# Attention of a hybrid decoder trunk: 128-column value products at the diagonal, and one split of the joined heads for each pair

## The chip, the cores and the metric

The kernel runs on one core of a Trainium2 chip. The metric is the device time of one launch in microseconds; lower is better. The engines are called PE (TensorE, matrix products), PEld (its weight loads), DVE (VectorE), ACT (ScalarE), POOL (GpSimd) and SP (SyncE, which issues the transfers here).

## The reference

Two layers, each with a token mixer and an MLP, on 1024 positions of width 1024. The part that matters here is the forgetting attention: 8 heads of width 64, a causal softmax with a bias made of running sums of the forget gates, and the product with the values.

```
def block(args):
    i, q_i, c_i = args
    scores = jnp.einsum('bqhd,bkhd->bhqk', q_i, k).astype(jnp.float32) * scale
    bias = c_i[..., :, None] - c[..., None, :]
    q_pos = i * Q_BLOCK + jnp.arange(Q_BLOCK)
    causal = key_pos[None, :] <= q_pos[:, None]
    logits = jnp.where(causal, scores + bias, -jnp.inf)
    p = jax.nn.softmax(logits, axis=-1)
    return jnp.einsum('bhqk,bkhd->bqhd', p.astype(v.dtype), v)
```

Beside it each layer has four heads of retention (a linear recurrence in chunks of 128), a joint output projection, two layer norms and an MLP of width 4096 with a squared ReLU. Everything is float32.

## The kernel before

A product of two float32 operands is made of three products in the type fp32r, a rounded float32: `split(hi, lo, src)` (L158) writes the rounded value with ACT (L161, a cast) and the rest with DVE (L162, a subtraction), and the three products hi·hi, hi·lo and lo·hi are added up in PSUM. Splitting an operand therefore costs one ACT and one DVE instruction.

A layer runs in stages: the value projection, retention, the projection of queries and keys, attention, the output projection, the MLP. The attention stage stands at about 315 to 492 us in layer 0 and at about 1515 to 1690 us in layer 1. In each layer it covers the 8 heads one after the other, each in 4 steps `qq` of 256 query rows, so a layer has 32 steps. Beside the steps runs other PE work as a filler (`take`): 18 items for each of the first 24 steps, the projections of queries and keys for the later pairs of heads, then 4 for each step, among them the transposes of the retention's result (`ret_transposes`, L488, tile `rl`). Within a stage `merge` interleaves three generators, and a scheduler then sets each engine's order; every engine works through its own queue in that order.

For a step, `front` makes the scores of two blocks of 128 rows (PE L541 and, for the causal mask, L545), adds the bias and takes the minimum (DVE L547), applies exp (ACT L553), takes the reciprocal of the sum (DVE L555) and normalises the probabilities in place (POOL L556, tile `sc`). `load_bias` loads the running sums of a head (SP L513, tile `ncb`, one buffer) and derives `ref` (POOL L515); `bias` makes the bias tile `rel` (POOL L522). So POOL carries `ref`, `rel` and `sc`.

`back` (L560) turns the probabilities: for two key blocks and two query blocks PE transposes four 128x128 blocks into one PSUM tile `tr` (L569), and `split` makes from it the pair `pt` (hi and lo, 128 partitions x 4 blocks, three buffers of each). At the diagonal one of the four blocks lies wholly above it. It is not transposed: the key blocks are taken in the other order, so that it becomes block 0, and POOL writes zeros there (L574, once for hi and once for lo). `values` (L580) then runs 2 key blocks x 2 halves (hi, lo), four matmuls of 256 columns (L592), five tiles later than `back`. Values are kept as hi and lo side by side, 64 + 64 columns of the stationary operand, so that one half of the PSUM partitions has the product with hi and the other that with lo. At the end of each second step both halves are joined: ACT copies one (L603), DVE adds the other (L604, tile `ot`), and `split` writes the 64 partitions of this head into `mix`, the operand of the output projection. Two heads make a pair, which fills 128 partitions of `mix`.

Of the kernel before, what the change touches and what calls it, by code (L numbers as in the profile page):

```python
# [9 lines left out]
F32 = mybir.dt.float32  # L10
# [7 lines left out]
P = 128  # L18
# [4 lines left out]
RH, RD = 4, 128  # L23
# [52 lines left out]
def hybrid_trunk(ctx: ExitStack, tc, x, w_in, w_out, w_ff1, w_ff2, ln1_g, ln1_b, ln2_g, ln2_b,  # L76
                 b_forget, ret_gn_g, cst_d, rope_d, out):
    nc = tc.nc
    A, V, G, PE, SP = nc.scalar, nc.vector, nc.gpsimd, nc.tensor, nc.sync
# [43 lines left out]
    def nm(s):  # L123
        uid[0] += 1
        return f"{s}_{uid[0]}"
# [33 lines left out]
    def split(hi, lo, src, scale=1.0):  # L159
        if scale == 1.0:  # L160
            A.copy(hi, src)  # L161
            V.tensor_tensor(lo, src, hi.bitcast(F32), op=ALU.subtract)  # L162
        else:
            A.mul(hi, src, scale)
            V.scalar_tensor_tensor(lo, src, scale, hi.bitcast(F32), op0=ALU.mult, op1=ALU.subtract)
# [85 lines left out]
    def transpose_in(dst, src, tt, groups=2, banks_of=None):  # L251
        for g in range(groups):
            if banks_of is None:
                tr = ps_tr.tile([P, 4, P], F32, tag="tr", name=nm("tr"))
            else:
                tr = banks_of().rearrange("p (a b) -> p a b", b=P)
            for j in range(4):
                PE.transpose(tr[:, j, :], src[:, (4 * g + j) * P : (4 * g + j + 1) * P], ident)
            o = (tt % 4) * P
            split(dst.tile(0, g, tt // 4)[:, :, o : o + P], dst.tile(1, g, tt // 4)[:, :, o : o + P], tr)  # L260
# [226 lines left out]

    def ret_transposes(mr, pool):  # L488
        for tt in range(NT):
            t = pool.tile([P, RH * RD], F32, tag="rl", name=nm("rl"), bufs=1)  # L490
            SP.dma_start(t, r_d[tt * P : tt * P + P, :])
            transpose_in(mr, t, tt, groups=1)
            yield

    def attention(pool, mixes, fill, need, take):
        pv, heads, sums, rels, pvq = {}, {}, {}, {}, []

        def load(h):
            qs = pool.tile([P, S], F32R, tag="qs", name=nm("qs"), bufs=2)
# [60 lines left out]
        def back(h, qq, probs):  # L560
            for jp in range(qq + 1):
                diag = jp == qq
                tr = ps_tr.tile([P, 4, P], F32, tag="tr", name=nm("tr"))
                js = (2 * jp + 1, 2 * jp) if diag else (2 * jp, 2 * jp + 1)
                for i, j in enumerate(js):
                    for rb in range(2):
                        if diag and i == 0 and rb == 0:
                            continue
                        PE.transpose(tr[:, 2 * i + rb, :], probs[rb][:, j * P : j * P + P], ident)  # L569
                pt = [pool.tile([P, 4, P], F32R, tag=f"pt{a}", name=nm("pt"), bufs=PT_BUFS) for a in range(2)]  # L570
                f = 1 if diag else 0
                if diag:
                    for a in range(2):
                        G.memset(pt[a][:, 0, :].bitcast(F32), 0.0)  # L574
                split(pt[0][:, f:4, :], pt[1][:, f:4, :], tr[:, f:4, :])
                pvq.append((h, qq, jp, js, pt))
                yield
                if len(pvq) > LAG:
                    values(*pvq.pop(0))
                    yield  # L580

        def values(h, qq, jp, js, pt):
            p, e = h // 2, h % 2
            diag = jp == qq
            hq = qq // 2
            if (h, hq) not in pv:
                pv[(h, hq)] = ps_pv.tile([P, 512], F32, tag="pv", name=nm("pv"))
            ob = pv[(h, hq)]
            vp = heads[h][2]
            for i, j in enumerate(js):  # L590
                for b in range(2):
                    PE.matmul(ob[:, (qq % 2) * 256 : (qq % 2) * 256 + 256], vp[:, j, :], pt[b][:, 2 * i : 2 * i + 2, :],  # L592
                              start=qq % 2 == 0 and jp == 0 and i == 0 and b == 0,
                              stop=qq % 2 == 1 and diag and i == 1 and b == 1)
            if qq % 2 == 1 and diag:
                if p not in mixes:
                    mixes[p] = act.tile([P, 2, S], F32R, tag="act", name=nm("mix"))
                m = mixes[p]
                own = slice(64 * e, 64 * e + 64)
                oth = slice(64 - 64 * e, 128 - 64 * e)  # L600
                hs = slice(512 * hq, 512 * hq + 512)
                ot = pool.tile([P, 512], F32, tag="ot", name=nm("ot"), bufs=1)
                A.copy(ot[own], ob[oth])  # L603
                V.tensor_tensor(ot[own], ot[own], ob[own], op=ALU.add)  # L604
                split(m[own, 0, hs], m[own, 1, hs], ot[own])

        steps = [(h, qq) for h in range(FH) for qq in range(4)]
        def merge(gens):
# [20 lines left out]
        for i, st in enumerate(steps):  # L629
            h, qq = st  # L630
            n = fill(h, qq)
            if h + 1 < FH:
                if qq == 0:
                    if h % 2 == 1:
                        need((h + 1) // 2)
                    load(h + 1)
                if qq == 3 - DEPTH:
                    load_bias(h + 1)
            gens = [(2 * (qq + 1), back(h, qq, probs[st]))]
            if i + DEPTH < len(steps):  # L640
                nx = steps[i + DEPTH]
                gens.append(fronts(nx, probs[nx]))
            if n:
                gens.append((n, take(n)))
            merge(gens)
            if i + DEPTH + 1 < len(steps):
                bias(*steps[i + DEPTH + 1])
        while pvq:
            values(*pvq.pop(0))

    def layer(l, xT, nxt):
# [44 lines left out]
        with tc.tile_pool(name=f"p2_{l}", bufs=1, reuse_waits="tile") as pool:  # L696
            def rest():
                for p in range(1, FH // 2):
                    yield from project_qk(l, p, xT, pool)
                yield from ret_transposes(mr, pool)  # L700

            work = rest()

            done = [0, 0.0]

            def fill(h, qq):
                done[1] += FILL[h] * (qq + 1) / 10
                return max(0, int(done[1]) - done[0])

            def take(n):  # L710
                for _ in range(n):
                    done[0] += 1
                    next(work, None)
                    yield

            def need(p):
                while done[0] < QK_STEPS * p:
                    done[0] += 1
                    next(work, None)

            attention(pool, mix, fill, need, take)
            for _ in work:
                pass
# [453 lines left out]
```

## Time and profile before

| | us |
|---|---|
| median of 3 runs | 2420.84 (2418.31 to 2422.09) |
| the profiled execution | 2424.44 |
| its span, first to last instruction | 2422.6 |
| PE busy | 2364.4 (98%) |
| DVE busy | 1520.2 (63%) |
| ACT busy | 1025.1 (42%) |
| POOL busy | 359.3 (15%) |

The mean granted clock of TensorE in the profiled execution is 0.996. Two views are read below beside the totals: windows, which give each engine's busy time in a stretch, and timelines, which list an engine's instructions in order, with the idle time before each in brackets and what ended it. A group of several instructions stands in one row with its count; its duration is then from the first start to the last end.

### The profile page before, as it was taken

The numbers are of one execution on the slowest core, as the hardware profiler recorded it, in microseconds if no ns is written. First come the engines' busy times: TensorE is split into PE (matmuls) and PEld (weight loads), VectorE is DVE, ScalarE is ACT, GpSimd is POOL, SyncE is SP. The second block draws the span as 40 slices with busy tenths as digits, with TensorE's granted clock in tenths as the row PEclk, the third lists the DMA queues.
The fourth block names the chain that finished last, engine by engine and source line by source line (L and its number), as shares of the span: only waits on it lengthen the run. The fifth ranks groups of instructions, "written<-read, shape, count | busy, mean of one in ns | idle before, by whom it ended". The sixth has DMA issues, their size and how long they took to land. (4 is left out here: it accounts for less than half of the span.)

```text
span 2422.6 us, 32508 instructions
## 1 busy us (share of the span) xinstructions
PE 2364.4 (98%) x11888; PEld 1984.5 (82%) x11888; DVE 1520.2 (63%) x2719; ACT 1025.1 (42%) x1572; POOL 359.3 (15%) x597
## 2 busy tenths in 40 slices
PE   8999998999999999999999999989999999999997
PEld 8888877787888888888898888877878888888886
DVE  4655446854876667665655553587557766576557
ACT  3222245744644453434321212477264444543331
POOL 0232234510000000000202322354000000000003
PEclk9999999999999999999999999999999999999999
DMA  7565765533354458677545567654334544586663
GB/s 232 175 217 196 234 201 150 138 114 121 100 193 178 148 187 289 219 208 220 188 157 187 209 213 237 181 166 114 118 105 148 185 167 161 206 292 216 198 193 147
DMA packets 243808, 442.48 MB, mean 183 GB/s; under 512 B 26032, under 2 KB 128432, under 8 KB 235456
## 3 DMA queue, kind: packets, MB, share of 16 engines
q1 hardware_dynamic: 241344, 432.01, 54.9%
q10 hardware_dynamic: 2304, 8.39, 0.8%
q8 instruction: 94, 1.54, 0.3%
q14 instruction: 66, 0.54, 0.1%
HBM read 301.85 MB, written 138.48 MB: 182 GB/s over the span
## 5 line engine op out<-in xcount | busy, mean ns | idle before, releaser
L162 DVE TENSOR_TENSOR elo<-est,ehi 128x1024 fp32r<-128x1024 f32 x216 | 261.1, 1223 | 182.7 <-ACT ehi L161 182.3
L161 ACT CAST ehi<-est 128x1024 fp32r<-128x1024 f32 x216 | 226.6, 1054 | 344.1 <-PE pv L1068 120.8
L286 POOL TENSOR_SCALAR sd<-mv 128x1 f32<-128x1 f32 x15 | 13.9, 927 | 1211.9 <-DVE mv L283 1211.6
L233 PE MATMUL mm<-whi,act 128*128 128x512 f32 (+1 forms) x608 | 187.2, 373 | 1.0 <-DVE act L162 0.5
L858 PE MATMUL qk<-xop,whi 128*128 128x512 f32 x608 | 187.2, 389 | 0.0
L233 PE MATMUL qk<-whi,act 128*128 128x512 f32 (+1 forms) x608 | 186.4, 373 | 0.8 <-DVE act L162 0.8
L161 ACT CAST whi<-wst 128x512 fp32r<-128x512 f32 (+1 forms) x140 | 115.8, 829 | 168.4 <-PE qk L233 36.0
L162 DVE TENSOR_TENSOR wlo<-wst,whi 128x512 fp32r<-128x512 f32 (+1 forms) x140 | 133.1, 954 | 40.4 <-ACT whi L161 39.7
L858 PE MATMUL pv<-xop,whi 128*128 128x512 f32 x512 | 157.7, 389 | 0.0
L592 PE MATMUL pv<-pt,vp 128*128 128x256 f32 x640 | 133.4, 310 | 13.1 <-POOL pt L574 12.4
L858 PEld LDWEIGHTS qk<-xop,whi 128*128 128x128 f32 x608 | 114.2, 188 | 23.6
L233 PEld LDWEIGHTS mm<-whi,act 128*128 128x128 f32 x608 | 111.8, 191 | 19.8 <-ACT whi L161 0.9
L233 PEld LDWEIGHTS qk<-whi,act 128*128 128x128 f32 x608 | 110.3, 189 | 18.6 <-DVE act L162 1.0
L233 PE MATMUL mm<-act,whi 128*128 128x512 f32 x384 | 123.0, 396 | 0.0
L162 DVE TENSOR_TENSOR pt<-tr,pt 128x512 fp32r<-128x512 f32 (+1 forms) x160 | 100.1, 630 | 35.0 <-ACT pt L161 34.3
L858 PE MATMUL mm<-xop,whi 128*128 128x512 f32 x384 | 118.5, 390 | 1.5 <-DVE xop L162 1.5
L161 ACT CAST pt<-tr 128x512 fp32r<-128x512 f32 (+1 forms) x160 | 86.0, 541 | 78.3 <-PE tr L569 71.2
L858 PE MATMUL qk<-xop,wlo 128*128 128x512 f32 x304 | 118.6, 390 | 0.0
L553 ACT ACTIVATE sc<-sc,mx 128x128 f32<-128x128 f32 (+7 forms) x128 | 99.4, 777 | 43.5 <-DVE mx L547 40.3
L233 PE MATMUL mm<-wlo,act 128*128 128x512 f32 (+1 forms) x304 | 113.2, 373 | 0.7 <-DVE wlo L162 0.7
L858 PEld LDWEIGHTS pv<-xop,whi 128*128 128x128 f32 x512 | 96.1, 188 | 19.9
L233 PE MATMUL qk<-wlo,act 128*128 128x512 f32 (+1 forms) x304 | 112.2, 369 | 0.0
(279 smaller groups left out, 5973.7 us busy)
## 6 DMA issues: line engine op xcount, KB each, us to landing
est<-h_d SPq DMA_DIRECT2D x224, 256.0 KB, 3.7
wst<-in_w_ff_dram SPq DMA_DIRECT2D x76, 512.0 KB, 4.3
wr<-in_w_ff_dram SPq DMA_DIRECT2D x32, 1024.0 KB, 5.0
t_d<-ts SPq DMA_DIRECT2D x32, 1024.0 KB, 4.2
h_d<-hs SPq DMA_DIRECT2D x32, 1024.0 KB, 5.6
est<-t_d SPq DMA_DIRECT2D x128, 256.0 KB, 3.9
h_d<-rest SPq DMA_DIRECT2D x32, 768.0 KB, 5.7
est<-in_w_ff_dram SPq DMA_DIRECT2D x96, 256.0 KB, 4.7
```

The source lines that it names most:

```text
L161: A.copy(hi, src)
L162: V.tensor_tensor(lo, src, hi.bitcast(F32), op=ALU.subtract)
L233: PE.matmul(ps, lhs(a, k), rhs(b, k), start=first and i == 0 and j == 0, stop=last and i == n - 1 and j == 2)
L286: G.tensor_scalar(sd, mv[:, :, 1], EPS, 1.0, op0=ALU.add, op1=ALU.mult)
L553: A.activation(sc[:, 0:ne], sc[:, 0:ne], AF.Exp, bias=mx, scale=-1.0, accum_out=sm)
L592: PE.matmul(ob[:, (qq % 2) * 256 : (qq % 2) * 256 + 256], vp[:, j, :], pt[b][:, 2 * i : 2 * i + 2, :], start=qq % 2 == 0 and jp == 0 and i ...
L858: PE.matmul(ps, ops[p][a][:, k, :], right[p][b][:, k, :], start=first and k == 0 and n == 0, stop=last and k == 3 and n == 2, skip_group_c ...
```

## The change

Three edits. At a diagonal the full key block now comes first, with matmuls of 256 columns, and the block that is half above the diagonal second, with matmuls of 128 columns that leave the other 128 columns as they are; the zeros are not written. `ot` is kept for a pair of heads in two tiles (`ot0`, `ot1`), each head fills its 64 partitions, and the split into `mix` is made for 128 partitions at the end of the second head. The tile `rl` shares a buffer (`ev2`) with the evictions of the query and key projection. The values matmul is at L591 in the kernel after.

```diff
@@ ret_transposes
-            t = pool.tile([P, RH * RD], F32, tag="rl", name=nm("rl"), bufs=1)
+            t = pool.tile([P, RH * RD], F32, tag="ev2", name=nm("rl"), bufs=1)
@@ attention
-        pv, heads, sums, rels, pvq = {}, {}, {}, {}, []
+        pv, heads, sums, rels, pvq, outs = {}, {}, {}, {}, [], {}
@@ back
                 f = 1 if diag else 0
-                if diag:
-                    for a in range(2):
-                        G.memset(pt[a][:, 0, :].bitcast(F32), 0.0)
                 split(pt[0][:, f:4, :], pt[1][:, f:4, :], tr[:, f:4, :])
@@ values
-            for i, j in enumerate(js):
+            for n, i in enumerate((1, 0) if diag else (0, 1)):
+                f = 1 if diag and n == 1 else 0
+                c = (qq % 2) * 256
                 for b in range(2):
-                    PE.matmul(ob[:, (qq % 2) * 256 : (qq % 2) * 256 + 256], vp[:, j, :], pt[b][:, 2 * i : 2 * i + 2, :],
-                              start=qq % 2 == 0 and jp == 0 and i == 0 and b == 0,
-                              stop=qq % 2 == 1 and diag and i == 1 and b == 1)
+                    PE.matmul(ob[:, c + f * P : c + 256], vp[:, js[i], :], pt[b][:, 2 * i + f : 2 * i + 2, :],
+                              start=qq % 2 == 0 and jp == 0 and n == 0 and b == 0,
+                              stop=qq % 2 == 1 and diag and n == 1 and b == 1)
@@ values, the join
-                ot = pool.tile([P, 512], F32, tag="ot", name=nm("ot"), bufs=1)
+                if e == 0:
+                    outs[hq] = pool.tile([P, 512], F32, tag=f"ot{hq}", name=nm("ot"), bufs=1)
+                ot = outs[hq]
                 A.copy(ot[own], ob[oth])
                 V.tensor_tensor(ot[own], ot[own], ob[own], op=ALU.add)
-                split(m[own, 0, hs], m[own, 1, hs], ot[own])
+                if e == 1:
+                    split(m[:, 0, hs], m[:, 1, hs], ot)
```

In the tables of order below an operation's line stands first, then what it writes and reads, with buffer numbers (they differ between the two kernels), and the shape. On POOL, where the bias of the head of index 4 is made in layer 0 (the sc of 384 to 768 columns belong to the second and third step of the head of index 3), this stood before:

```order
L556 TENSOR_SCALAR sc_3923<-sc_3923,ri_3932 128x384
L515 TENSOR_SCALAR ref_4109<-ncb_4107 128x4
L522 TENSOR_SCALAR rel_4172<-ncb_4107,ref_4109 128x256
L522 TENSOR_SCALAR rel_4244<-ncb_4107,ref_4109 128x512
L556 TENSOR_SCALAR sc_3957<-sc_3957,ri_3966 128x512
L574 MEMSET pt_3939 128x128
L556 TENSOR_SCALAR sc_4057<-sc_4057,ri_4085 128x640
L574 MEMSET pt_3940 128x128
L522 TENSOR_SCALAR rel_4329<-ncb_4107,ref_4109 128x768
L574 MEMSET pt_4051 128x128
L574 MEMSET pt_4052 128x128
L556 TENSOR_SCALAR sc_4088<-sc_4088,ri_4102 128x768
```

and this stands there now:

```order
L556 TENSOR_SCALAR sc_3893<-sc_3893,ri_3902 128x384
L556 TENSOR_SCALAR sc_3925<-sc_3925,ri_3934 128x512
L515 TENSOR_SCALAR ref_4075<-ncb_4073 128x4
L522 TENSOR_SCALAR rel_4136<-ncb_4073,ref_4075 128x256
L522 TENSOR_SCALAR rel_4204<-ncb_4073,ref_4075 128x512
L556 TENSOR_SCALAR sc_4023<-sc_4023,ri_4051 128x640
L522 TENSOR_SCALAR rel_4286<-ncb_4073,ref_4075 128x768
L556 TENSOR_SCALAR sc_4054<-sc_4054,ri_4068 128x768
```

The four memsets are gone, and the sc of 512 columns has moved ahead of `ref`, the instruction that needs the transfer of ncb.

On PE, at a diagonal of the head of index 3, the values matmuls and what follows them were

```order
L592 MATMUL pv_4227<-pt_4135,vp_3638 128x256
L592 MATMUL pv_4227<-pt_4134,vp_3638 128x256
L592 MATMUL pv_4227<-pt_4135,vp_3638 128x256
L541 MATMUL qk_4318<-ks_4039,qs_4037 128x512
L541 MATMUL qk_4318<-ks_4042,qs_4037 128x512
```

(the fourth stands a little ahead of them), and now they are

```order
L591 MATMUL pv_4187<-pt_4101,vp_3617 128x256
L591 MATMUL pv_4187<-pt_4100,vp_3617 128x128
L591 MATMUL pv_4187<-pt_4101,vp_3617 128x128
L591 MATMUL pv_4245<-pt_4143,vp_3617 128x256
L541 MATMUL qk_4275<-ks_4007,qs_4005 128x512
L541 MATMUL qk_4275<-ks_4010,qs_4005 128x512
```

Two of the four matmuls have 128 columns. On all of PE's queue the count of instructions stays the same, and outside the attention stage so does their order.

On DVE, at a join of the head of index 3, the second of its pair, the queue before was

```order
L604 TENSOR_TENSOR ot_4272<-ot_4272,pv_4227 64x512
L162 TENSOR_TENSOR pt_4210<-tr_4205,pt_4209 128x384
L547 ISA sc_4351,mx_4365<-qk_4361,rel_4329,mx_4355 128x320
L547 ISA mx_4365 128x1
L555 RECIPROCAL ri_4326<-sm_4324 128x1
L162 TENSOR_TENSOR pt_4252<-tr_4246,pt_4251 128x512
L547 ISA sc_4372,mx_4376<-qk_4373,rel_4329 128x512
L547 ISA mx_4376 128x1
L162 TENSOR_TENSOR mix_3894<-ot_4272,mix_3894 64x512
```

and is now, at the same place,

```order
L605 TENSOR_TENSOR ot_3867<-ot_3867,pv_4187 64x512
L162 TENSOR_TENSOR pt_4172<-tr_4167,pt_4171 128x384
L555 RECIPROCAL ri_4283<-sm_4281 128x1
L547 ISA sc_4306,mx_4320<-qk_4316,rel_4286,mx_4310 128x320
L547 ISA mx_4320 128x1
L162 TENSOR_TENSOR pt_4212<-tr_4206,pt_4211 128x512
L547 ISA sc_4327,mx_4331<-qk_4328,rel_4286 128x512
L547 ISA mx_4331 128x1
L162 TENSOR_TENSOR mix_3866<-ot_3867,mix_3866 128x512
```

The subtraction for mix has 128 partitions instead of 64; at the joins of a pair's first head there is none any more.

## Rows read from the trace of the kernel before

**Rows 1.** Page, part 1: busy us, share of span, instructions.

```profile
PE 2364.4 (98%) x11888; PEld 1984.5 (82%) x11888; DVE 1520.2 (63%) x2719; ACT 1025.1 (42%) x1572; POOL 359.3 (15%) x597
```

**Rows 2.** Page, part 4: chain that ended last, share of the span by engine.

```profile
PE 30%; DVE 2%; POOL 1%; ACT 1%; issue 0%; DMA 0%; DVEq 0%; ACTq 0%; POOLq 0%
```

**Rows 3.** Waits of PE: line <- releaser, us in total, times, longest.

```profile
PE pv L592 <- POOL pt L574: 12.4, 11, 2.4
PE tr L569 <- DVE pt L162: 7.2, 11, 1.2
...
PE tr L569 <- POOL sc L556: 1.5, 3, 0.9
```

**Rows 4.** Windows: busy of PE, PEld, DVE, ACT, POOL; clock, DMA share, GB/s.

```profile
300.00:400.00 100.00, 97.49 (x526) 81.10 (x524) 51.07 (x131) 45.74 (x92) 31.87 (x58) 0.98 0.63 185
400.00:500.00 100.00, 87.37 (x592) 72.91 (x593) 81.58 (x237) 71.15 (x153) 52.16 (x100) 0.98 0.48 130
...
1600.00:1700.00 100.00, 89.37 (x614) 74.03 (x613) 83.71 (x245) 74.20 (x158) 52.95 (x103) 1.00 0.48 130
```

**Rows 5.** Windows of 25 us, same columns.

```profile
425.00:450.00 25.00, 23.10 (x171) 19.16 (x170) 23.72 (x71) 21.58 (x50) 14.46 (x28) 1.00 0.66 179
...
1625.00:1650.00 25.00, 22.77 (x165) 18.88 (x163) 23.42 (x71) 20.55 (x46) 12.78 (x27) 1.00 0.59 147
```

**Rows 6.** Windows where head 4's bias is made, both layers.

```profile
418.00:421.50 3.50, 1.08 (x4) 0.60 (x5) 0.00 (x0) 0.00 (x0) 3.50 (x8) 1.00 0.00 0
421.50:424.80 3.30, 3.30 (x17) 3.22 (x16) 2.05 (x4) 1.94 (x4) 1.87 (x5) 0.50 0.64 202
...
1615.00:1618.00 3.00, 0.78 (x4) 0.29 (x2) 1.53 (x5) 1.15 (x3) 3.00 (x9) 1.00 0.01 3
```

**Rows 7.** Timeline of POOL there, layer 0: start, us, instruction, idle before.

```profile
416.56 0.20 POOL L515 TENSOR_SCALAR ref<-ncb 128x4 f32<-128x4 f32 x1 [4.86 <-DMA ncb<-c_d]
...
417.97 0.69 POOL L556 TENSOR_SCALAR sc<-sc,ri 128x512 f32<-128x512 f32 x1
...
419.70 0.91 POOL L522 TENSOR_SCALAR rel<-ncb,ref 128x768 f32<-128x768 f32 x1
420.55 0.35 POOL L574 MEMSET pt<- 128x128 f32 x2
420.87 0.91 POOL L556 TENSOR_SCALAR sc<-sc,ri 128x768 f32<-128x768 f32 x1
```

**Rows 8.** Timeline of PE there, layer 0.

```profile
418.87 0.38 PE L592 MATMUL pv<-pt,vp 128*128 128x256 f32 x1 [2.44 <-POOL pt L574]
420.81 0.38 PE L592 MATMUL pv<-pt,vp 128*128 128x256 f32 x1 [1.56 <-POOL pt L574]
...
425.36 0.23 PE L545 MATMUL qk<-mbf,ibf 128*128 128x128 bf16 x1
425.42 0.61 PE L569 MATMUL tr<-cst,sc 128*128 128x128 f32 x4
```

**Rows 9.** Timeline of PE at the same place in layer 1.

```profile
1615.95 0.38 PE L592 MATMUL pv<-pt,vp 128*128 128x256 f32 x1 [0.67 <-POOL pt L574]
1617.89 0.39 PE L592 MATMUL pv<-pt,vp 128*128 128x256 f32 x1 [1.56 <-POOL pt L574]
```

**Rows 10.** Instructions of tile ot: ns min/median/max, first and last start.

```profile
L162 DVE TENSOR_TENSOR mix<-ot,mix x32: 662/689/1485, 345.3 to 1727.7; 64x512 fp32r<-64x512 f32 x32
```

**Rows 11.** Timeline of PE: three runs of equal matmuls.

```profile
251.42 0.60 PE L422 MATMUL tr<-tqk 128*128 128x128 f32 x4
...
354.75 0.60 PE L569 MATMUL tr<-cst,sc 128*128 128x128 f32 x4
...
361.27 0.87 PE L592 MATMUL pv<-pt,vp 128*128 128x256 f32 x6
```
**Rows 12.** Matmuls of two lines: ns min/median/max, first and last start, forms.

```profile
L592 PE MATMUL pv<-pt,vp x640: 274/282/562, 330.0 to 1725.0; 128*128 128x256 f32 x160
...
L569 PE MATMUL tr<-cst,sc x576: 270/273/422, 320.9 to 1719.3; 128*128 128x128 f32 x192
```

## Prediction

> **What bounds the kernel now.** I read the totals first. PE is busy for 2364.4 us, 98% of the span [rows 1], and in the chain that ended last the other engines have 2%, 1% and 1% [rows 2]. So only what shortens PE's queue or fills its gaps can move the end; of POOL's memsets and DVE's subtractions only the part counts that PE waits for. The list of PE's waits says where that is: 12.4 us in 11 waits of values matmuls for the zeros of L574, 7.2 us in 11 waits of transposes for the split of pt on DVE, 1.5 us for the normalised probabilities from POOL [rows 3]. Then the windows, for the stage. In the first 100 us window of attention in layer 0 PE is busy 97.49 of 100 with DVE at 51.07: PE is the bound there. In the window after it PE has 87.37 and DVE 81.58; in the same place of layer 1 PE has 89.37 and DVE 83.71 [rows 4]. So the early heads, which have the projections as filler, are bound by PE, and the late heads by PE, DVE and POOL in turn, DVE in front for a part: 23.72 and 23.42 of 25 us [rows 5].
>
> The worst place is the same in both layers: where the bias of head 4 (counted from 0) is made. From 418.0 to 421.5 us DVE and ACT do nothing, POOL is busy all the time and PE for 1.08 of 3.5 us [rows 6]. The timelines say why. POOL waited 4.86 us for ncb, and after `ref` at 416.56 it works off the rel, sc and memsets one after the other, up to the sc of 768 columns, which begins at 420.87 [rows 7]; PE's next values matmuls need the zeros, at 418.87 after 2.44 us of waiting and at 420.81 after 1.56 us [rows 8]. Right behind these gaps the granted clock is 0.50, that is 1.2 GHz, from 421.5 to 424.8, with PE busy for all 3.30 us [rows 6]. In layer 1 the same waits are 0.67 and 1.56 us [rows 9], and no clock falls there (1.00 in that window, [rows 6]).
>
> **The change part by part.** The sum is made against the profiled execution, 2424.44 us, of which the span is 2422.6; it lies 3.6 us above the median of 2420.84, and I take that off at the end.
>
> *The zeros, place of head 4.* In layer 0 three things go: 2.44 and 1.56 us of waits, and half of 3.30 us, since the same instructions at full clock take 1.65: together 5.65. Next late is POOL's chain. After `ref` at 416.56 it still makes the two rel (until 417.97), sc of 640 columns (an estimate of 0.8, between the 0.69 of 512 columns and the 0.91 of 768), rel of 768 (0.91) and sc of 768 (0.91) [rows 7], so it ends at about 420.6. The transposes that read it begin at 425.42 in the trace [rows 8]; PE would be there at 425.42 − 5.65 = 419.8. So 0.8 us of the gain is lost to this wait: −4.8. The sc of 512 columns, which the first transposes behind the waits read, is no hindrance, since it now stands ahead of `ref`. In layer 1 the two waits, −2.2, with POOL in the same relation.
>
> *The zeros, the other seven waits.* 12.4 − 2.44 − 1.56 − 0.67 − 1.56 = 6.2 us [rows 3, 8, 9]. A wait for the zeros ends when POOL reaches the memset, behind rel and sc in its queue; without it PE reaches the next transposes earlier, and these read sc from the same queue or wait for the split of pt on a DVE that is busy for 94% of such a stretch [rows 5]. Bounds: 0 (all of it comes back as those waits) and −6.2. I take a third, −2.1, by the nearest case, nearer to the lower gain, since the 7.2 us of waits for DVE and 1.5 us for sc [rows 3] show that both are often later than PE already.
>
> *The split of mix once for a pair.* An instruction costs the same for 64 and 128 partitions as far as its 512 columns set it, so of 32 subtractions of 0.689 us [rows 10] 16 go, 11.0 us of DVE; as many casts go on ACT, which has slack. It counts only where DVE is the bound. PE's loss to DVE is 7.2 us in all [rows 3]; the two stretches of 25 us with DVE at 94% or more [rows 5] hold about one pair each, so two subtractions of a pair, 4 × 0.69 = 2.8 us at most, of which I take half: −1.4. Bounds 0 and −2.8. The one subtraction of 1.485 us [rows 10] was beside work of POOL; one such less is within this.
>
> *The 128-column matmuls.* At each diagonal 2 of the 4 values matmuls go from 256 to 128 columns: 2 × 4 steps × 8 heads × 2 layers = 128. A 256-column one takes (0.87 − 0.28)/5 = 0.118 us from start to start (a run of six, [rows 11]; 0.28 is the median length of one, [rows 12]). An fp32r matmul with fewer than 256 columns doesn't stand in this trace: the scores of 128 columns are computed 256 wide, and 640 is cut into 320 + 320. So bounds by neighbours. Below: the bf16 mask of 128 columns hands over after 0.06 us (425.36 to 425.42, [rows 8]): 128 × (0.06 − 0.118) = −7.4 us. Next: the float32 transposes of 128 columns, (0.60 − 0.27)/3 = 0.11 us [rows 11, 12]: −1.0. Above: a plain float32 matmul of 128 columns stands in the trace as two records of 0.11 us each (the row of L422 holds two matmuls in four records, [rows 11]), 0.22 us: +13.1. I take 0.11, the transposes: they load a stationary operand of the same kind each time, and their pace does not follow their columns (128 at 0.11, 256 at 0.118), so that a load of weights seems to set both. Half of the 128 lie in the early heads, where PE is the bound: −0.5.
>
> The Trainium skill, page "TensorE: Matmul & The Clock Gate", section "Back-to-back issue gap", gives about 81 ns for a matmul of 128 columns in a stream with weight loads, and about 56 ns without them. By 81 ns the term would be 128 × (81 − 118) = −4.7 us instead of −1.0. The transposes' 0.11 us speaks against it for 4-byte operands. That is a rival of its own, below, whose time goes by rows.
>
> *The order.* The change moves a few hundred of PE's instructions in the first four heads of a layer, where PE is busy 97%: 0 to +1, I take +0.4. On SP the first load of rl now stands ahead of ncb of head 4; an issue is some 0.3 to 0.5 us, and POOL waited 4.86 us for ncb there [rows 7]. If ncb comes 0.5 us later, `ref` and the chain behind it do, in two layers: bounds 0 and +1, I take +0.5. The buffer that rl now shares with evictions is free by the time it is needed, as the projection ends before.
>
> Sum: −4.8 − 2.2 − 2.1 − 1.4 − 0.5 + 0.9 = −10.1. So 2424.44 − 10.1 = 2414.3, and less the 3.6: 2411 us for the median.
>
> **The rivals.**
>
> *Narrow fp32r matmuls are as slow as plain float32 (0.22 us).* +13.1 us of PE time. For it: the trace never shows one under 256 columns, and 4-byte operands at 128 columns do take 0.22 us in the one product where they aren't transposes. Against it: the transposes. In the early heads nothing hides it, 64 × (0.22 − 0.118) = +6.5. In the late heads PE then fills gaps in which it would wait for DVE or POOL: the gains from the seven other waits and from DVE (2.1 + 1.4 = 3.5) fall away, and between none and half of the other 6.5 is hidden. Sum: −7.0 (place of head 4) + 6.5 + 3.3 to 6.5 + 0.9 = +3.7 to +6.9; with the 3.6 off, 2424.5 to 2427.7, about 2426: slower. If the late heads also keep the 3.5, it is 2421 to 2424, no change. The point from which it turns: with a sum of −9.6 without this term, the narrow matmul must cost 0.118 + 9.6/128 = 0.19 us to cancel them.
>
> *The waits only move.* The zeros go, but PE waits at the next transposes for sc or pt almost as long; the lost clock and half of the other 4 us in layer 0 stay won, 1.65 + 2.0 = some 3.5. For it: `ref` waits for ncb as before, and everything behind it on POOL. Against it: sc of 512 is now ahead of `ref`, and POOL sheds the memsets between. 2424.44 − 3.5 − 3.6 = 2417.3 with nothing from the other terms, and 2419 with +1 from the order: no change to just faster.
>
> *Columns set the pace of narrow matmuls.* At 0.06 us as in the mask, −7.4 us in place of −1.0, a half to all of it felt: 2411 − 3 to − 6 = about 2406. For it only the bf16 row; against it the transposes.
>
> **How the numbers follow.** What a measurement of this kernel can tell from no change is about 0.2%, 4.8 us: faster is under 2416.0, slower above 2425.7. Chances: the forecast 0.47, of which 0.43 faster and 0.04 same; slow narrow matmuls 0.32, of which 0.17 same, 0.13 slower and 0.02 faster; moved waits 0.14, of which 0.10 same, 0.02 faster, 0.02 slower; columns 0.04, faster; the rest, a new order that goes badly, 0.03, slower. So faster 0.51, same 0.31, slower 0.18. The forecast's own range: the seven waits and DVE between their bounds (−9.0 to 0 about the −3.5 taken) give 2406 to 2415. The whole range reaches up over the moved waits and most of the slow matmuls: 2404 to 2426.
>
> **What the profile after would show.** PE waits for no memset; at the place of head 4 DVE and ACT no longer stand still, and no window there has a clock of 0.50. The pace of a run of 128-column values matmuls is 0.11 us; 0.2 us or more would make the fourth step wrong and the first rival right, 0.06 us the last one. In the late heads, PE's waits for DVE's pt and POOL's sc together stay below 8.7 + 4.1 us (the two thirds of 6.2 that come back); if they exceed 8.7 + 8, the waits only moved. DVE is busy about 11 us less. A change of the time in stages outside attention by more than 1 us would make the whole frame wrong, since PE's order there is as before.

## The result and the profile after

The changed kernel takes 2403.93 us (median of 4 runs, 2402.20 to 2406.83) against 2421.47 us before in the same comparison: ratio 0.9929, 95% interval 0.9914 to 0.9945, that is 13 to 21 us less. A second comparison later gave 2404.72 against 2424.76 us, ratio 0.9914 (0.9899 to 0.9929). Forecast were 10 us. The profiled execution took 2406.83 us with a span of 2404.8, against 2424.44 and 2422.6.

The totals of the page after, to be set against [rows 1]: PE is busy for 3.3 us less, DVE for 10.2 us less, POOL for 22.3 us less.

```profile
PE 2361.1 (98%) x11888; PEld 1983.0 (82%) x11888; DVE 1510.0 (63%) x2703; ACT 1015.2 (42%) x1556; POOL 337.0 (14%) x469
```

Since the span fell by 17.8 us and PE's work only by 3.3, most of the gain is idle time of PE. The list of PE's waits after (us in total, times, longest) says the same; against [rows 3] the 12.4 us for the zeros are gone, and 7.2 us for DVE have become 3.4:

```profile
PE tr L569 <- DVE pt L162: 3.4, 4, 0.9
PE tr L569 <- POOL sc L556: 2.1, 3, 1.4
...
PE qk L541 <- DVE mx L547: 1.5, 2, 0.8
```

The windows after (busy PE, PEld, DVE, ACT, POOL, clock, DMA share, GB/s) answer to [rows 4]: PE went from 87.37 to 94.23 and from 89.37 to 96.38 of 100 us in the windows of the late heads. A small part of this is that the stage ends earlier, by some 10 us in layer 0, and more of the output projection falls into the window.

```profile
400.00:500.00 100.00, 94.23 (x639) 79.57 (x639) 81.01 (x238) 70.55 (x153) 46.68 (x63) 0.98 0.48 134
...
1600.00:1700.00 100.00, 96.38 (x655) 81.56 (x654) 77.10 (x220) 67.88 (x145) 42.58 (x59) 1.00 0.43 123
```

At the place where head 4's bias is made, POOL's timeline after has no memset and no sc of 512 behind `ref`, as the order said [rows 7]:

```profile
415.13 0.20 POOL L515 TENSOR_SCALAR ref<-ncb 128x4 f32<-128x4 f32 x1 [5.35 <-DMA ncb<-c_d]
415.43 1.15 POOL L522 TENSOR_SCALAR rel<-ncb,ref 128x256 f32<-128x256 f32 x2
416.55 0.80 POOL L556 TENSOR_SCALAR sc<-sc,ri 128x640 f32<-128x640 f32 x1
417.33 0.91 POOL L522 TENSOR_SCALAR rel<-ncb,ref 128x768 f32<-128x768 f32 x1
418.21 1.90 POOL L556 TENSOR_SCALAR sc<-sc,ri 128x768 f32<-128x768 f32 x2
```

PE there, to be set against [rows 8], waits for these sc of 640 and 768 columns:

```profile
417.41 0.33 PE L569 MATMUL tr<-cst,sc 128*128 128x128 f32 x1 [0.43 <-POOL sc L556]
419.17 0.55 PE L569 MATMUL tr<-cst,sc 128*128 128x128 f32 x3 [1.44 <-POOL sc L556]
```

So the next wait is the one that the prediction named, only longer: 1.87 us instead of 0.8. And in this execution the slow clock is still there. The windows after [rows 6]:

```profile
418.00:420.00 2.00, 0.83 (x7) 0.83 (x8) 0.43 (x4) 0.33 (x3) 2.00 (x3) 1.00 1.09 358
420.00:425.00 5.00, 5.00 (x30) 4.28 (x28) 3.48 (x12) 3.63 (x11) 3.71 (x6) 0.66 0.98 267
```

A mean clock of 0.66 over 5 us with PE busy throughout is about the same loss as before (0.34 of 5 us: 1.7).

### The profile page after: what moved, and what is told of

Same layout as the page of the kernel before. It is cut to its first block, busy times and chain, and to the rows that moved or that the text cites. A ratio compares the mean times of both kernels' runs of the same rounds, so it can differ in the third digit from the quotient of the medians.

```text
span 2404.8 us, 32463 instructions
## 1 busy us (share of the span) xinstructions
PE 2361.1 (98%) x11888; PEld 1983.0 (82%) x11888; DVE 1510.0 (63%) x2703; ACT 1015.2 (42%) x1556; POOL 337.0 (14%) x469
## 4 chain that ended last, share of the span: by engine, by line
PE 88%; DMA 4%; DVE 4%; ACT 1%; issue 1%; SPq 0%; POOL 0%; DVEq 0%; ACTq 0%; POOLq 0%
PE mm L233 17%; PE qk L233 11%; PE qk L860 9%; PE tr L1070 7%; PE pv L1070 7%; PE pv L860 7%; PE qk L1070 5%; PE mm L1070 5%; PE mm L860 5%; PE tr L860 4%; PE tr L569 2%; PE qk L541 2%; PE pv L591 2%; DMA q_d<-ev 1%; PE pv L233 1%
## 5 line engine op out<-in xcount | busy, mean ns | idle before, releaser
L591 PE MATMUL pv<-pt,vp 128*128 128x256 f32 (+1 forms) x640 | 127.5, 302 | 0.2
L556 POOL TENSOR_SCALAR sc<-sc,ri 128x128 f32<-128x128 f32 (+7 forms) x128 | 96.8, 762 | 136.7 <-DVE ri L555 104.8
```

The costliest lines, as they stand in the source:

```text
L556: G.tensor_scalar(sc[:, 0:ne], sc[:, 0:ne], ri, 1.0, op0=ALU.mult, op1=ALU.mult)
L591: PE.matmul(ob[:, c + f * P : c + 256], vp[:, js[i], :], pt[b][:, 2 * i + f : 2 * i + 2, :], start=qq % 2 == 0 and jp == 0 and n == 0 and ...
```

## The experiments

The ratio of each run is to the kernel before, measured beside it. The first four tell the edits apart.

**The zeros alone.** The edits in `back` and `values` of the diff; mix, ot and rl as before.

```diff
-                if diag:
-                    for a in range(2):
-                        G.memset(pt[a][:, 0, :].bitcast(F32), 0.0)
...
+            for n, i in enumerate((1, 0) if diag else (0, 1)):
+                f = 1 if diag and n == 1 else 0
```

> The kernel before with the first edit alone: no memsets, full key block first, 128-column matmuls for the half block; mix is split for each head as before. Theory: the gain of 17 us comes from the zeros (13 us of waits that do not come back) and from the matmuls' shorter time (about 4 us), so this alone gives 2404 to 2407 us, and no wait of PE for POOL's pt is left. Rival: the fewer subtractions on DVE carry a third of the gain; then 2409 to 2412 us, and the late heads show more waits of transposes for DVE's pt than the changed kernel's 3.4 us.

Measured: 2410.76 us, ratio 0.9954 (0.9939 to 0.9970). It is two thirds of the gain. No values matmul waits for POOL any more; PE's wait of the transposes for DVE is 3.6 us, that of the scores for DVE's mx 2.8 us. By its time the rival was right, that the pair split carries a third.

**The pair split alone.** The edits of `ot`, mix and rl; memsets and 256 columns stay.

```diff
+                if e == 0:
+                    outs[hq] = pool.tile([P, 512], F32, tag=f"ot{hq}", name=nm("ot"), bufs=1)
+                ot = outs[hq]
...
+                if e == 1:
+                    split(m[:, 0, hs], m[:, 1, hs], ot)
```

> The kernel before with the other two edits alone: mix split once for a pair of heads, rl in the buffer of the evictions; the memsets and the matmuls of 256 columns stay. Theory: at most 2 us, 2418 to 2422 us; the waits for the memsets stay at about 12 us. Rival (DVE carries a third): 2414 to 2416 us, with the waits of transposes for DVE's pt falling from 7.2 to below 4 us.

Measured: 2407.8 us, ratio 0.9937 (0.9924 to 0.9949). Both theories expected far less. This edit alone brings about as much as the zeros alone, and it also takes waits away that are listed under the zeros: the row of the zeros in its list of waits, to be set against 12.4 in [rows 3], with the one for DVE:

```profile
PE pv L592 <- POOL pt L574: 6.9, 8, 1.4
...
PE tr L569 <- DVE pt L162: 2.9, 8, 0.8
```

The two gains overlap: 12 and 15 us apart, 17 to 20 together. PE's order differs from that of before here too, so a part of the 15 us may be order.

**Wide matmuls without zeros.** The half block's matmuls read blocks 1 and 2 of pt, so the product of that block is not the reference's.

```diff
-                    PE.matmul(ob[:, c + f * P : c + 256], vp[:, js[i], :], pt[b][:, 2 * i + f : 2 * i + 2, :],
+                    PE.matmul(ob[:, c : c + 256], vp[:, js[i], :], pt[b][:, 2 * i + f : 2 * i + 2 + f, :],
```

> The changed kernel, but the half block's matmuls are 256 columns wide again and write all 256 output columns; they read blocks 1 and 2 of pt in place of blocks 1 alone, so no zeros are needed and nothing waits for any (this product is not the reference's). The price of the narrow matmuls alone. Theory: the first narrow one of a pair takes 0.06 us, the second 0.109, against 2 x 0.118: +0.067 us x 64 = +4.3 us of PE time, a part of it in gaps, so 2406 to 2408.5 us. Rival (the prediction's step, 0.11 us each): +1.0 us, 2404 to 2405.5 us.

Measured: 2398.33 us, ratio 0.9904 (0.9890 to 0.9918). Wide matmuls are not slower than narrow ones; both expectations had the sign wrong. That they are faster is not settled, since the interval overlaps with the changed kernel's, barely with the first (0.9914 to 0.9945) and by more with the second (0.9899 to 0.9929).

**All diagonal matmuls narrow.** Each wide matmul of a diagonal's full block becomes two of 128 columns.

```diff
+                    for u in ((f,) if f else (0, 1)) if diag else (None,):
+                        lo, hi = (0, 2) if u is None else (u, u + 1)
+                        PE.matmul(ob[:, c + lo * P : c + hi * P], vp[:, js[i], :], pt[b][:, 2 * i + lo : 2 * i + hi, :],
```

> The changed kernel, but the full key block of a diagonal is also computed in 128-column matmuls, two in place of each of 256: six narrow ones in a row. Theory: a load of weights can start 0.108 us after the one before at the soonest; only the first narrow one behind a wide one finds its load done and takes 0.06 us; a run of six takes 0.06 + 5 x 0.109 = 0.605 us, against 0.118 x 2 + 0.06 + 0.109 = 0.405 now: +0.20 us x 64 = +12.8 us of PE time, of which the gaps of the late heads hide up to a third: 2412 to 2417 us. Rival (a narrow one takes 0.06 us, always): six take 0.36 us, -3 us: 2400 to 2402 us.

Measured: 2406.88 us, ratio 0.9939 (0.9926 to 0.9951): 2 to 3 us above the changed kernel, less than expected. The timeline of PE shows six narrow ones in a row between transposes and scores:

```profile
489.08 0.60 PE L569 MATMUL tr<-cst,sc 128*128 128x128 f32 x4
489.44 0.86 PE L593 MATMUL pv<-pt,vp 128*128 128x128 f32 x6
490.13 0.45 PE L541 MATMUL qk<-ks,qs 128*128 128x512 f32 x1
```

From the start of the six to the start of the next it is 0.69 us, 0.115 each: the pace of the transposes, half of plain float32's 0.22. So the pace I expected was right for runs of narrow matmuls, and a part of their extra time seems to fall into gaps: the total of PE's waits for DVE's pt is 1.9 us here and for POOL's sc 1.1, against 3.4 and 2.1 in the changed kernel.

The next four ask what in each edit does it.

**The changed kernel with a split for each head.**

```diff
-                if e == 1:
-                    split(m[:, 0, hs], m[:, 1, hs], ot)
+                split(m[own, 0, hs], m[own, 1, hs], ot[own])
```

> The changed kernel, but mix is split for each head again (16 more casts on ACT and 16 more subtractions on DVE); the two ot tiles and the shared buffer of rl stay. PE's order is that of the changed kernel but for 22 rows. If DVE's load in the late heads sets the gain of the pair edit: 2408 to 2411 us, as with the zeros alone (2410.8). If the second ot buffer or the order sets it: 2403 to 2405 us.

Measured: 2410.64 us, ratio 0.9953 (0.9936 to 0.9970), the same as with the zeros alone. It is the count of splits, not the buffers and not PE's order. PE's waits here, against 3.4 and 1.5 in the changed kernel:

```profile
PE tr L569 <- DVE pt L162: 6.0, 6, 1.1
...
PE qk L541 <- DVE mx L547: 2.9, 4, 0.8
```

**The block order alone.** Before, with the full block's two matmuls ahead of the half block's.

```diff
-            for i, j in enumerate(js):
+            for n, i in enumerate((1, 0) if diag else (0, 1)):
```

> The kernel before, with only the order of the two key blocks at a diagonal changed: the full block first, the half block with its zeros second, all 256 columns wide. The order of all engines is else that of before. PE needs the zeros 0.24 us later at each diagonal, 11 waits: about -2 us, 2418 to 2422 us, if the zeros themselves are what is late; the same 12 us of waits but for this.

Measured: 2415.3 us, ratio 0.9963 (0.9950 to 0.9976): 6 to 12 us, where I expected 2. The zeros are still written and read, and the wait for them is down from 12.4 us:

```profile
PE pv L593 <- POOL pt L574: 4.5, 4, 2.0
...
PE tr L569 <- POOL sc L556: 2.2, 4, 1.0
```

The 0.24 us that I expected was the time of two matmuls. But the four do not stand together in PE's queue. PE's timeline before, at the place of [rows 8], shows one values matmul at 418.87, and its three fellows only behind scores and transposes:

```profile
421.61 1.06 PE L569 MATMUL tr<-cst,sc 128*128 128x128 f32 x4
422.32 0.99 PE L592 MATMUL pv<-pt,vp 128*128 128x256 f32 x3
```

The one that stands ahead read the zeros; with the full block first, the zeros are read by the last two of the four, 3.8 us later here. (The matmul at 420.81 is likewise the first of the next diagonal, whose fellows start at 423.60.)

**One ncb for all heads.** The bias of heads 1 to 7 is wrong.

```diff
+            if h == 0:
+                ncb = pool.tile([P, S], F32, tag="ncb", name=nm("ncb"), bufs=1)
+                SP.dma_start(ncb, rows(c_d[h], P))
+            else:
+                ncb = sums[0][0]
```

> The changed kernel, but ncb is loaded for head 0 of a layer alone and serves all 8 heads (the bias of the others is wrong): POOL's ref never waits for a transfer after that. PE's order is that of the changed kernel but for 28 rows. If the chain rel, transfer of ncb, ref, rel, sc sets what is left at the place of head 4 (1.9 us of waits and 1.7 us of lost clock in layer 0): 2398 to 2401 us. If the waits only move on to DVE: 2403 to 2405 us.

Measured: 2401.74 us, ratio 0.9915 (0.9898 to 0.9932): 2 us below the changed kernel's first median, between the two expectations and inside the noise of the comparison. So the transfer that POOL waits for is worth 2 us or so now, if anything. A second buffer for ncb, which would do this for each head's own sums, was not tried: it needs 4 KB in each partition, and the tiles leave less.

**Two ot tiles alone.** Before, with the two tiles and the shared buffer of rl, but a split for each head.

```diff
-                ot = pool.tile([P, 512], F32, tag="ot", name=nm("ot"), bufs=1)
+                if e == 0:
+                    outs[hq] = pool.tile([P, 512], F32, tag=f"ot{hq}", name=nm("ot"), bufs=1)
+                ot = outs[hq]
```

> The kernel before with two ot tiles and the shared buffer of rl, but mix split for each head, memsets and 256 columns as before; PE's order is that of before but for 8 rows, DVE's, ACT's and POOL's are unchanged. If the single ot tile held back the joins: 2408 to 2412 us. If it is the count of DVE's instructions or the order that came with it: 2419 to 2423 us.

Measured: 2423.56 us, ratio 1.0001 (0.9989 to 1.0013). The buffers alone are worth nothing that can be measured, 3 us at most either way.

The last four: a version without the narrow matmuls, DVE against ACT, and a way to relieve DVE further.

**Pair split and block order, zeros and wide matmuls kept.** The pair split alone, and in `values`:

```diff
-            for i, j in enumerate(js):
+            for n, i in enumerate((1, 0) if diag else (0, 1)):
```

> The kernel before with mix split once for a pair, two ot tiles and the full key block first at a diagonal; the memsets stay and all matmuls are 256 wide. It computes what the reference does. The order of PE, DVE and ACT is exactly that of the run with wide matmuls and no zeros (2398.3 us), so the difference to it is the price of the memsets with the full block first. If the block order had already taken most of the waits for zeros and the narrow matmuls are worth nothing: 2399 to 2403 us, at or below the changed kernel's 2404. If the zeros still cost what they cost with one split for each head (the 4.5 us between 2415.3 and 2410.8): 2403 to 2406 us.

Measured: 2404.49 us, ratio 0.9916 (0.9902 to 0.9929); the changed kernel beside it 2404.72, ratio 0.9914. All that the change gives is here, with all memsets and no narrow matmul. By its time the second expectation held, that the zeros still cost something. Against the run with wide matmuls and no zeros, the comparison that the expectation names, the memsets cost some 3 us by the ratios (0.9916 against 0.9904) and 6 by the medians of two comparisons, but the intervals overlap, so it isn't settled. If they do cost that, the narrow matmuls cost the changed kernel as much as the missing memsets give it. The zeros' waits:

```profile
PE pv L593 <- POOL pt L574: 2.8, 7, 0.8
PE tr L569 <- DVE pt L162: 1.8, 4, 0.8
```

**DVE's part of the split alone.** 16 subtractions more on DVE, no more casts on ACT.

```diff
+                if e == 0:
+                    V.tensor_tensor(m[own, 1, hs], ot[own], ot[own], op=ALU.subtract)
+                else:
+                    split(m[:, 0, hs], m[:, 1, hs], ot)
```

> The changed kernel with 16 more DVE subtractions of 64x512 (at the first head of a pair, into mix, overwritten later), and no more casts on ACT: DVE's work is that of a split for each head, ACT's that of one for a pair. If DVE is what the split for each head costs: 2408 to 2411 us. If it is ACT: 2403 to 2405 us.

Measured: 2412.92 us, ratio 0.9953 (0.9941 to 0.9966), 8.2 us above the changed kernel beside it. DVE's part alone is enough, without ACT's. PE's order differs from the changed kernel's in many more rows here than with the split for each head (22 rows), so a part of the 8 us may be order; there it was 6 to 7 us by the medians, 6 to 9 by the ratios. The waits of PE that grew, from 3.4 and 1.5:

```profile
PE tr L569 <- DVE pt L162: 5.5, 10, 0.9
PE qk L541 <- DVE mx L547: 3.8, 9, 0.8
```

**The changed kernel once more,** for the two comparisons above.

> The changed kernel once more, for a comparison on the same chip with the two others of this call: 2402 to 2406 us.

Measured: 2404.72 us, ratio 0.9914 (0.9899 to 0.9929).

**The remaining subtractions on POOL.**

```diff
-                    split(m[:, 0, hs], m[:, 1, hs], ot)
+                    A.copy(m[:, 0, hs], ot)
+                    G.tensor_tensor(m[:, 1, hs], ot, m[:, 0, hs].bitcast(F32), op=ALU.subtract)
```

> The changed kernel with mix's 16 remaining subtractions moved from DVE to POOL (by POOL's 0.73 us for 128x256 an estimate of 1.45 us each). It computes what the reference does. If DVE's load is what the late heads pay for, as 16 added subtractions for 8 us say: 2397 to 2400 us. If POOL's queue, with sc behind the new instruction, is as late as DVE by now: 2403 to 2407 us.

Measured: 2406.63 us, ratio 0.9936 (0.9920 to 0.9952), no gain. The waits for DVE's pt fall, and POOL takes their place: its queue holds sc back longer, and the output projection waits for the last piece of mix.

```profile
PE tr L569 <- POOL sc L556: 3.1, 3, 1.7
PE mm L233 <- POOL mix L608: 2.8, 2, 1.5
...
PE tr L569 <- DVE pt L162: 1.6, 6, 0.3
```

No run with the reference's output is faster than the changed kernel; the version with the pair split, zeros, wide matmuls and the block order equals it.

## Why the prediction was right or wrong

The direction was right, and the frame: PE bound, all of the gain in the attention stages. The median of 2403.93 us lies at the lower edge of the whole range (2404 to 2426) and below the forecast's own (2406 to 2415). In the trace the order number of a PE instruction in the MLP of layer 0 comes 10.6 us earlier after the change, and all later ones keep this until the attention of layer 1 adds 7 us. The size was too small, 10 us against 17, by one term above all, and by the clock.

*The split of mix, −1.4 forecast, 6 to 9 us measured* (the changed kernel against the split for each head, and against the added subtractions; with the zeros still in place the pair split gave 12 to 18). This is the failed step. I capped it by PE's listed waits for DVE, 7.2 us, and counted only the two stretches where DVE was at 94%. The list names the last releaser alone. By the order of the queues a late DVE also makes exp, reciprocal and so POOL's sc and memsets late, and these stood in the list under POOL: the pair split alone took 5.5 of the 12.4 us of waits for zeros. A second way stands in the last section: a subtraction of mix also holds POOL's sc back when it starts first. No run separates the two. The saving of DVE's time was near the forecast (10.2 us of 11.0), and at least half of it came out at the end.

*The zeros, −4.8 − 2.2 − 2.1 = −9.1 forecast, 7 to 15 us measured by the edit alone.* The size was right, the mechanism only in part. By the medians, more than half of it comes not from leaving the zeros out but from reading them last (8 of 12 us): the block order alone gives 6 to 12 us, and with the pair split beside it the version that keeps the memsets equals the changed kernel. My text counted the order of the blocks at nothing; it saw that the values matmuls at 418.87 and 420.81 waited for the zeros, and not that each stood alone, 2.8 to 3.5 us ahead of its three fellows, so that the block order could put the reading off. At the place of head 4 the rest went differently: the wait for sc is 1.87 us instead of 0.8, and the 1.65 us of slow clock, which I had as won, stay in the profiled execution. Of the other seven waits I let two thirds come back. In the sum over the stage nothing came back: with the zeros alone PE's waits for DVE's pt, act and mx and POOL's sc in this stage add up to 3.6 + 1.6 + 2.8 + 2.0 = 10.0 us, against 7.2 + 0.2 + 1.0 + 1.5 = 9.9 before.

*The narrow matmuls, −0.5 forecast: no gain measured*, and between nothing and 6 us of loss against the run with wide ones. The pace of 0.11 us was right; the row of six has 0.115. Rival 1 (0.22 us) and the rival of 0.06 us are both refuted by it for runs of such matmuls. The Trainium skill, page "TensorE: Matmul & The Clock Gate", section "Back-to-back issue gap", gave some 81 ns for this case; the trace doesn't agree, with its 115 ns. By the starts of single instructions in the trace after, the first narrow one behind a wide one gives way after 0.06 us, the second after 0.11; but over both layers, against the run with wide matmuls, the values matmuls take some 2.3 us less and the scores of L541 some 2.3 us more, from start to start and without waits, so what is spared seems to be given back behind them.

*The order, +0.9 forecast.* No run has the changed kernel's order with the work of the kernel before, so it wasn't measured by itself; a loss doesn't show. A gain does, in the profiled pair: at the start of the stage in layer 0, ahead of the first zeros and the first join, PE waited before

```profile
320.88 0.55 PE L569 MATMUL tr<-cst,sc 128*128 128x128 f32 x3 [0.93 <-POOL sc L556]
322.79 0.80 PE L233 MATMUL mm<-act,wlo 128*128 128x512 f32 x1 [1.36 <-DVE ev L162]
```

and after, with the scores and transposes a little later among the projections,

```profile
321.75 0.50 PE L233 MATMUL mm<-act,wlo 128*128 128x512 f32 x1 [0.22 <-DVE ev L162]
```

With the clock below, 3.8 of the 10.6 us of layer 0 come here, by PE's order numbers 1600 to 1900. In the trace of the changed kernel's second run, with the same order, it is only 1.5, so a part of the 17.8 us between the two profiled spans is luck of the execution.

*The clock, −1.65 forecast, within the −4.8.* My text read one fall of the granted clock in the kernel before, from 421.5 us. Its trace has a second one that I overlooked, 0.50 from 322.5 to 325.9 us, right behind the two waits just shown; the clock of 0.98 in the first window of [rows 4] comes from it, and after the change that window has 1.00:

```profile
300.00:400.00 100.00, 99.01 (x544) 82.36 (x542) 52.44 (x136) 46.91 (x93) 29.47 (x41) 1.00 0.64 187
```

So the profiled execution before lost 2 x 1.7 us in this stage, the one after 1.7, and the second run's nothing (its clock is 1.00 from 420 to 425 us). Over all executions with a recorded clock its mean is 0.9954 for the kernel before (54, by comparison 0.9950 to 0.9958) and 0.9972 for the changed one (8). Of 2424 and 2405 us that is some 11 and 7 us lost, of which a fall at the very end of the program takes some 5.5 in the traces of both. By this estimate 4 to 5 us of the 17 to 20 come from PE running less at the lower level.

*The rival of moved waits* (only 3.5 us) is refuted by the trace: PE's listed waits in this stage shrank by more than the 12.4 us. What remains open: whether wide matmuls without memsets are truly faster than the changed kernel, since this run's order differs from it in several hundred rows of PE and the intervals overlap.

## What to carry to other kernels

Where a loop of several engines is tight, a wait in the profile's list belongs to the last releaser only; where an engine is as busy as DVE here (82 to 84% of a window), a large part of an instruction's time can reach the end, whichever engine the waits are put down to; test it by adding the same instruction once more. Before removing an operation that is waited for, see whether its first reader can go last: the reordering of two matmuls gave some 8 of the 12 us that the removal gave. A matmul with half the columns need not take half the time: here 0.115 us in a row against 0.118. And compare the granted clock of all runs, not of one profile: with the waits some falls of the clock went too here.

## What the runs showed of the hardware

A DVE subtraction that reads two SBUF tiles took 0.69 us alone and up to 1.49 us when a POOL instruction had started shortly before. In the trace before, the sc of POOL starts at 504.59 and ends at 505.72, and the subtraction that starts at 504.77 ends 0.54 us after that. The same 0.53 to 0.54 us stand behind all 19 subtractions of mix in the traces before and after that took over 1 us, each of which started behind a POOL instruction that reads SBUF:

```profile
504.59 1.13 POOL L556 TENSOR_SCALAR sc<-sc,ri 128x1024 f32<-128x1024 f32 x1 [1.20 <-DVE ri L555]
```

```profile
504.77 1.49 DVE L162 TENSOR_TENSOR mix<-ot,mix 64x512 fp32r<-64x512 f32 x1 [0.28 <-ACT mix L161]
```

After the change the same holds for 128 partitions, whose median rose to 1.09 us (rows of the tile, against [rows 10]); beside POOL's memsets alone it was not prolonged (0.69 us, twice in the run with two ot tiles alone). The other way round, before, an sc of 384 columns that started 0.17 us behind a subtraction of mix took 0.95 us, where the median is 0.59.

```profile
L162 DVE TENSOR_TENSOR mix<-ot,mix x16: 681/1093/1449, 376.2 to 1710.2; 128x512 fp32r<-128x512 f32 x16
```

The Trainium skill, page "SBUF — State Buffer", section "Who interferes with whom", says that a DVE instruction with two SBUF inputs and a GpSimd instruction that reads SBUF exclude each other, whichever is first, and that one that only writes does not count. The traces agree, with the 1.49 and 0.95 us beside a reading POOL instruction and the 0.69 us beside memsets. In all, the 32 subtractions before took 28.2 us and the 16 after 16.4. The 11.8 us less are near the 11.0 of the forecast by luck: it reckoned all at the median of 0.69, while the mean was 0.88 us before and 1.02 after.
